# Expert gathers shifted from the V stages to the U stages, and ten modulation parts made inside the first layer's attention

## The chip, the core and the metric

The kernel runs on one core of one Trainium2 chip. The metric is device time in microseconds (us), the median of several runs. The core's engines work side by side: TensorE (PE in the rows; PEld is its weight loads) multiplies matrices, VectorE (DVE) and ScalarE (ACT) do elementwise work, GpSimd (POOL) does some elementwise work and here issues the indirect loads, and SyncE (SP) issues nearly all other transfers. Each engine takes its instructions strictly in the order in which they were placed, and waits where one is not ready. Sixteen DMA engines move data between the chip's memory and the on-chip buffers; they are shared by all transfers.

## What is computed

The program is two layers of a generator with 512 latent and 256 context tokens of width 1024. Cut to what matters here:

```
for l in range(2):
    mod = silu(c) @ w_mod[l] + b_mod[l]          # six parts of 1024: sh1 sc1 g1 sh2 sc2 g2
    h   = rms_norm(x) * norm_mix * (1 + sc1) + sh1
    y   = concat(windowed attention A, neighbourhood attention B, RWKV-7 scan C)(h @ w_in) @ w_out
    x   = x + g1 * y
    h2  = rms_norm(x) * norm_ffn * (1 + sc2) + sh2
    # PEER: 8 heads, each picks 16 of 16384 experts per token
    act = gelu(h2 . u[expert])
    x   = x + g2 * sum(gate * act * v[expert])
```

In layer 0 the context tokens (256) go through all of it too, in layer 1 only latent tokens do. Each of the six parts is made for `c` and for `c_ctx`, so one part needs a 1024 x 1024 slice of `w_mod` (4 MB) and little arithmetic.

## The kernel before

The tokens lie in six tiles of 128: LAT = 0 to 3, CTX = 4 and 5. A layer runs through `project` (norm, input projection), `mix` (scan, attention, output projection) and `peer`.

`peer` treats most tokens densely: for every one of the 16384 experts. The U stage goes through 128 blocks of 128 experts, two blocks (a pair) per row of `uT` (1 MB): `pa = u . h2`, 48 matmuls a pair, split into high and low parts (`uH`, `uL`, `hH`, `hL`) for precision. Between the pairs it makes the gate matrix W (`choose`, then `gates`: 32 steps a token tile, each two `oh` and one `og` on VectorE, eight `pw` matmuls and one copy), stored through `wscr`. The gate work of all tiles has to end at group GSPREAD of 32, since its buffers then make room for the results of the last blocks (`late`). The V stage goes through the same blocks again: `y += (gate * act) . v`, 64 pairs of a 1 MB row of v each. I call these stages U0, V0 (layer 0) and U1, V1 (layer 1).

The remaining tokens (CTX in layer 0, LAT tile 3 in layer 1) are not done densely: class `Gather` fetches the chosen expert rows. A gather is one indirect DMA on GpSimd's queue that brings one row of u and v for each of 128 tokens (1 MB). Two gathers together are then worked off by VectorE (L1464, the product with h; L1470, the sum into `accc`). There are 256 gathers in layer 0 and 128 in layer 1. They share six buffers (`row`) with the rows of `uT` and v. When a gather is placed is set by `tick`, called once per pair: every call adds NTICK[layer][place] to a sum, and each whole unit of it places one gather with high priority. The places are 0 (five calls in `scores`), 1 (U stage, groups below NFIRST), 2 (U stage, from NFIRST on), 3 (V stage). What is left at the end of the V stage is placed by `flush`.

`mod_unit` makes one modulation part: eight loads `wmod` of 512 KB, 32 small matmuls, a bias and, for the parts that the norms use, a transpose. In layer 0 parts 0 and 1 are made first in `project`, parts 2 to 5 behind them, with lower priority. Parts 0 and 1 of layer 1 are made in layer 0's `attention`, by `fill`, called once per head step there (a head step is one call of `soft`: 48 in layer 0, 8 for A on CTX, 8 for B on CTX, 16 for B, 16 for A on LAT; B on CTX does not call `fill`). Parts 2 to 5 of layer 1 are made in layer 1's `project`.

The order on every engine is not written by hand: the instructions are placed when the program is built, in the order in which a model of the chip finds them ready, highest priority first. So a change of one number moves instructions elsewhere too. In `mix` of layer 0 the context's output projection and its PEER choice (`outproj_ctx`, `peer_ctx`) have a higher priority than attention, which fills in between, and the latent output projection (`outproj`) needs all of attention.

Of the kernel before, what the change touches and what calls it, by code (L numbers as in the profile page):

```python
# [16 lines left out]
PSUM = bass.MemoryType.PSUM  # L17
# [17 lines left out]
LATER = 2000  # L35
NROW = 6
NQ = 2
MOFF = 500
GSPREAD = (24, 20)
LATE = (28, 28)  # L40
NM1 = 2
NMW = (6, 4)
NRAW = 4
TC0 = 6
NPSC, NPSL = 2, 4
# [9 lines left out]
NPRT = 4  # L55
NQKB = {"qs": 3, "kh": 3, "kl": 2}

NTICK = ((1, 1.0, 1.5, 2.4), (0, 0, 1.06, 1.06))
NFIRST = (12, 3)
FEATS = (12, 13, 4, 0, 5, 1, 6, 2, 7, 3, 14, 8, 9, 10, 11)  # L60
LAT = (0, 1, 2, 3)
# [5 lines left out]
class Kernel:  # L67
    nw = 0

    def __init__(self, ctx, tc, i, out, dbg):  # L70
        self.ctx, self.tc, self.nc, self.i, self.out, self.dbg = ctx, tc, tc.nc, i, out, dbg
        self.cp = ctx.enter_context(self.pool(name="cp", bufs=1))
        self.mods = list(range(NM1))

        self.xsb = {}
        self.consts()
        self.scratch()
# [150 lines left out]
    def project(self, l, st):  # L228
        tc, nc, i = self.tc, self.nc, self.i
        wc = l == 0  # L230
        cpl = self.colp[l]
        hp_ = st.enter_context(self.pool(name="hp", bufs=1))
        hH = hp_.tile([P, KC, T], F32R, name="hH")
        hL = hp_.tile([P, KC, T], F32R, name="hL")
        def mods(chunks):
            if s3.pools is None:
                s3.pools = [s3.enter_context(self.pool(name="mp", bufs=NMW[l], side="right")),
                            s3.enter_context(self.pool(name="mps", bufs=2, space=PSUM, side="right"))]
            self.mod(l, chunks, *s3.pools)

        def src(t):
            if l == 0:
                return i["x"][t * P:(t + 1) * P] if t < 4 else i["ctx"][(t - 4) * P:(t - 3) * P]
            return self.xp[t * P:(t + 1) * P]
        with ExitStack() as s3:
            s3.pools = None
            if l == 0:
                mods(range(2))
            with ExitStack() as s2:
                np_ = s2.enter_context(self.pool(name="np", bufs=2))  # L250
                nps = s2.enter_context(self.pool(name="nps", bufs=2, space=PSUM))
                mc = self.mcol[:, l, 0]
                for tiles in (CTX, LAT[:2], LAT[2:]):
                    self.norm_T(src, mc, hH, hL, tiles, np_, nps)
            if l:
                self.gat.close()
            with self.tc.high_priority(offset=-MOFF):
                mods(range(NM1 if l else 2, 6))
        ps = st.enter_context(self.pool(name="pps", bufs=2, space=PSUM))
        psn = st.enter_context(self.pool(name="psn", bufs=2, space=PSUM, side="right"))  # L260
        xp_ = st.enter_context(self.pool(name="xp", bufs=1, side="right"))
        win = i["w_in"][l].rearrange("(k p) n -> p k n", p=P)
        pre = st.enter_context(self.pool(name="pre", bufs=1)).tile([P, KC, 256], F32, name="pre")
        with ExitStack() as s2:
            b2 = s2.enter_context(self.pool(name="b2", bufs=2))
            pb = s2.enter_context(self.pool(name="pb", bufs=1))
            with self.tc.high_priority(offset=PREO):
                nc.sync.dma_start(pre, win[:, :, QKV0:QKV0 + 256])
            last = self.features(l, s2, win, hH, hL, ps, psn, xp_, b2, pb)
        with ExitStack() as s2:  # L270
            self.qkv(l, s2, win, hH, hL, ps, psn, pre)
        last()
# [291 lines left out]
    def attention(self, l, st):  # L564

        nc, i = self.nc, self.i
        wc = l == 0
        ap = st.enter_context(self.pool(name="ap", bufs=1))
        a2 = st.enter_context(self.pool(name="a2", bufs=2))
        psl = st.enter_context(self.pool(name="psl", bufs=NPSL, space=PSUM))  # L570
# [4 lines left out]
        mp = st.enter_context(self.pool(name="mp", bufs=2))  # L575

        def fill():
            if self.mods:
                self.mod_unit(1, self.mods.pop(0), mp, psl, "pl")

        def soft(parts, h, use_sink):

# [62 lines left out]
        def heads_A(tiles, lat):  # L645
            k0_ = 0 if lat else NLAT
            q0 = tiles[0] * P
            for e in range(2):
                o = a2.tile([P, NLAT], F32, name="o")[:, :len(tiles) * P]
                hd = load_k(2, e, k0_)  # L650
                qs = [load_q(z, e, q0, (tiles[-1] + 1) * P) for z in range(2)]
                for a, t in enumerate(tiles):
                    k0, k1 = max(0, t - 1), min(3, t + 1)
                    nk = (k1 - k0 + 1) * P if lat else 0
                    vals = [va[:, 4 + z, e * 64:e * 64 + 64] for z in range(2)]
                    if lat:
                        vals = [va[:, z, e * 64:e * 64 + 64] for z in range(k0, k1 + 1)] + vals
                    prTs = []
                    for z in range(2):
                        pl = psl.tile([P, 512], F32, name="pl")  # L660
                        parts = [(pl, nk + 256)] if nk <= 256 else [(pl, nk), (psl.tile([P, 512], F32, name="pl"), 256)]
                        pc, n = parts[-1]
                        q = qs[z][:, a * P:(a + 1) * P]
                        qk_mm(pc[:, n - 256:n], q, hd, lambda x: x[:, NLAT - k0_:])
                        if lat:
                            qk_mm(pl[:, 0:nk], q, hd, lambda x: x[:, k0 * P:(k1 + 1) * P])
                            if k0 < t:
                                nc.vector.tensor_tensor(pl[:, 0:P], pl[:, 0:P], am[:, 0], OP.add)
                            if k1 > t:
                                nc.vector.tensor_tensor(pl[:, nk - P:nk], pl[:, nk - P:nk], am[:, 1], OP.add)  # L670
                        fill()
                        prTs.append(soft(parts, 2 * e + z, True))
                    weigh(pl, prTs, [vals] * 2, o[:, a * P:(a + 1) * P])
                keep(e, o, q0)
# [5 lines left out]
        if wc:  # L680
            heads_A(CTX, False)
            for c in range(2):
# [3 lines left out]
                for a in range(2):  # L686
                    prTs = []
                    for z in range(2):
                        pl = psl.tile([P, 512], F32, name="pl")
# [15 lines left out]
        for c in range(2):  # L705
            o = a2.tile([P, NLAT], F32, name="o")
            qs = [load_q(3 + c, z, 0, NLAT) for z in range(2)]
            hd = [load_k(5 + c, z, 0) for z in range(2)]
            for j in range(4):
                prTs = []  # L710
                for z in range(2):
                    h = 2 * c + z
                    bias = a2.tile([P, 256], F32, name="bias")
                    nc.sync.dma_start(bias, i["rpb"][l, h, :, j])
                    nc.gpsimd.tensor_tensor(bias, bias, bm[:, j], OP.add)
                    pl = psl.tile([P, 512], F32, name="pl")
                    qb = a2.tile([P, P], F32R, name="qb")
                    nc.gpsimd.tensor_copy(qb.rearrange("p (r w) -> p r w", w=16),
                                          qs[z].rearrange("p (r w) -> p r w", w=64)[:, :, 16 * j:16 * j + 16])
                    qk_mm(pl[:, 0:256], qb, hd[z],  # L720
                          lambda x: x[:, :NLAT].rearrange("p (r w) -> p r w", w=64)[:, :, reg[j]:reg[j] + 32])
                    qk_mm(pl[:, 256:512], qb, hd[z], lambda x: x[:, NLAT:])
                    nc.vector.tensor_tensor(pl[:, 0:256], pl[:, 0:256], bias, OP.add)
                    fill()
                    prTs.append(soft([(pl, 512)], h, False))
                weigh(pl, prTs, [[vb[:, j, y, h * 64:h * 64 + 64] for y in range(2)] +
                                 [vc[:, y, h * 64:h * 64 + 64] for y in range(2)] for h in (2 * c, 2 * c + 1)],
                      o.rearrange("p (r w) -> p r w", w=64)[:, :, 16 * j:16 * j + 16])
            keep(2 + c, o, 0)
# [691 lines left out]
class Gather:  # L1421
# [51 lines left out]
    def tick(self, z):  # L1473
        self.due += NTICK[self.l][z]
        while self.due >= 1 and self.todo:
            self.due -= 1
            with self.K.tc.high_priority(offset=100000):
                self.gather(*self.todo.pop(0))
# [75 lines left out]
```

## Time and profile before

| | us |
|---|---|
| median of three runs | 5100.41 (5096.14 to 5110.7) |
| profiled execution, its own time | 5089.21 |
| span of the profiled execution | 5087.4 |
| PE busy in the span | 4438.3 (87%) |
| DVE busy in the span | 3738.1 (73%) |

The profiled execution lies 11.2 us below the median, and 1.8 us of its time lie outside the span. From the span's start the stages lie about as follows (read from the trace): projection of layer 0 to 510, scan to 727, attention and the context's part beside it to 995, `outproj` and `scores` to 1150, U0 to 2062, V0 to 2839, projection of layer 1 from 2885, scan to 3574, attention to 3640, U1 to 4520, V1 to 5080.

### The profile page before, as it was taken

What the parts mean: (1) busy time and instruction counts of PE and PEld (TensorE: products, weight loads), DVE (VectorE), ACT (ScalarE), POOL (GpSimd) and SP (SyncE); (2) the same over time, 40 slices, a digit from 0 to 9 for tenths busy, and PEclk for the clock granted to TensorE, in tenths of its full rate; (3) what the DMA queues carried; (4) which work ended last, traced back from release to release, by engine and by line L of the source; (5) the groups of instructions that cost most, each with busy time, mean ns of one, the idle gap of its engine ahead of it and who ended that gap; (6) DMA issues with size and microseconds to landing.
All of it is one profiled execution on the core that took longest, in us unless ns stands there. A gap on an engine that the chain in (4) does not pass through costs nothing. (4 is left out here: it accounts for less than half of the span.)

```text
span 5087.4 us, 74067 instructions
## 1 busy us (share of the span) xinstructions
PE 4438.3 (87%) x27525; PEld 3679.1 (72%) x27525; DVE 3738.1 (73%) x7611; ACT 1731.5 (34%) x2881; POOL 1338.2 (26%) x1403
## 2 busy tenths in 40 slices
PE   7778797689999979898889596799698998988999
PEld 4558666567888867787777364687578997977887
DVE  3964658869967754798888867758589877556887
ACT  3433234333333322222222244324333443332333
POOL 0536632011111111232222235455011111112121
PEclk9779887799999989999999787779799998999999
DMA  7434665235777755899999942573424887567998
GB/s 273 134 104 125 190 203 177 90 128 197 250 260 283 281 217 214 305 372 371 367 364 368 349 162 87 131 204 111 157 100 170 305 296 278 215 236 256 342 357 299
DMA packets 573865, 1186.55 MB, mean 233 GB/s; under 512 B 63152, under 2 KB 376384, under 8 KB 520768
## 3 DMA queue, kind: packets, MB, share of 16 engines
q1 hardware_dynamic: 507072, 758.39, 44.8%
q0 software_dynamic: 61440, 418.41, 22.1%
q10 hardware_dynamic: 4992, 5.02, 0.3%
q8 instruction: 216, 3.54, 0.3%
q14 instruction: 145, 1.19, 0.1%
HBM read 1005.19 MB, written 176.50 MB: 232 GB/s over the span
## 5 line engine op out<-in xcount | busy, mean ns | idle before, releaser
L1453 POOL DMA_INDIRECT row<-in_uv,eidx x384 | 580.2, 1511 | 2465.2 <-DVE accc L1470 1369.1
L136 PE MATMUL pa<-hH,uL 128*128 128x512 f32 (+1 forms) x2048 | 757.9, 370 | 36.0 <-DVE uL L1313 35.9
L134 PE MATMUL pa<-hH,uH 128*128 128x512 f32 (+1 forms) x2048 | 754.5, 368 | 25.8 <-ACT ar L1317 21.6
L135 PE MATMUL pa<-hL,uH 128*128 128x512 f32 (+1 forms) x2048 | 752.4, 367 | 0.0
L135 PE MATMUL py<-vL,GH 128*128 128x512 f32 x1792 | 705.9, 394 | 26.6 <-DVE vL L1365 26.5
L136 PE MATMUL py<-vH,GL 128*128 128x512 f32 x1792 | 698.4, 391 | 0.0
L134 PE MATMUL py<-vH,GH 128*128 128x512 f32 x1792 | 625.2, 397 | 67.5 <-ACT vH L1363 44.1
L1464 DVE SCALAR_TENSOR_TENSOR row<-row,h2c 128x1024 f32<-128x1024 f32 x384 | 467.6, 1220 | 293.6 <-DMA row<-in_uv,eidx 293.3
L1470 DVE SCALAR_TENSOR_TENSOR accc<-row,dt,accc 128x1024 f32<-128x1024 f32 x384 | 491.6, 1280 | 5.4
L1311 ACT CAST uH<-row 128x1024 fp32r<-128x1024 f32 x256 | 268.5, 1050 | 653.7 <-PE pa L135 582.2
L136 PEld LDWEIGHTS pa<-hH,uL 128*128 128x128 f32 x2048 | 391.4, 191 | 84.8 <-DVE uL L1313 45.8
L134 PEld LDWEIGHTS py<-vH,GH 128*128 128x128 f32 x1792 | 340.9, 191 | 148.6 <-ACT vH L1363 53.4
L134 PEld LDWEIGHTS pa<-hH,uH 128*128 128x128 f32 x2048 | 391.6, 191 | 66.6 <-ACT ar L1317 22.2
L135 PEld LDWEIGHTS pa<-hL,uH 128*128 128x128 f32 x2048 | 390.9, 191 | 39.4
L135 PEld LDWEIGHTS py<-vL,GH 128*128 128x128 f32 x1792 | 341.3, 190 | 105.6 <-DVE vL L1365 34.5
L1313 DVE TENSOR_TENSOR uL<-row,uH 128x1024 fp32r<-128x1024 f32 x256 | 311.8, 1220 | 128.4 <-ACT uH L1311 127.5
L136 PEld LDWEIGHTS py<-vH,GL 128*128 128x128 f32 x1792 | 339.6, 189 | 70.7
L1370 ACT CAST GH<-G 128x512 fp32r<-128x512 f32 (+1 forms) x256 | 145.0, 567 | 637.7 <-PE py L135 414.9
L1365 DVE TENSOR_TENSOR vL<-row,vH 128x1024 fp32r<-128x1024 f32 x256 | 309.4, 1218 | 26.5 <-ACT vH L1363 26.5
L1363 ACT CAST vH<-row 128x1024 fp32r<-128x1024 f32 x256 | 262.5, 1043 | 41.7 <-DMA row<-in_uv 23.1
L1239 PE MATMUL pw<-og,oh 128*128 128x128 f16 x1792 | 237.7, 297 | 33.5 <-DVE og L1234 23.5
L1231 DVE TENSOR_TENSOR oh<-iota,ix 128x512 f16<-128x512 f16 x448 | 170.5, 419 | 104.8 <-PE pw L1239 103.9
(385 smaller groups left out, 8577.1 us busy)
## 6 DMA issues: line engine op xcount, KB each, us to landing
row<-in_uT SPq DMA_DIRECT2D x128, 1024.0 KB
row<-in_uv SPq DMA_DIRECT2D x128, 1024.0 KB
wscr<-W SPq DMA_DIRECT2D x28, 2048.0 KB
wmod<-in_w_mod SPq DMA_DIRECT2D x96, 512.0 KB
wt<-wscr SPq DMA_DIRECT2D x32, 1024.0 KB
row<-in_wq SPq DMA_DIRECT2D x24, 1024.0 KB
ascr<-aw SPq DMA_DIRECT2D x96, 256.0 KB
av<-ascr SPq DMA_DIRECT2D x48, 512.0 KB
```

Source lines behind the costliest of these rows:

```text
L134: mm(out, lh, rh, start=first, stop=False)
L135: mm(out, lh, rl, start=False, stop=False)
L136: mm(out, ll, rh, start=False, stop=last)
L1231: nc.vector.tensor_tensor(oh[:, z], self.iota4, ix[:, z, tt].unsqueeze(1).to_broadcast([P, P, 4]), OP.is_equal)
L1239: nc.tensor.matmul(pw[:, q], oh[:, 1, :, q], og[:, z, :, q], start=z == 0, stop=z == 1)
L1311: nc.scalar.copy(uH, ur)
L1313: nc.vector.tensor_tensor(uL, ur, uH.bitcast(F32), OP.subtract)
L1363: nc.scalar.copy(vH, vr)
L1365: nc.vector.tensor_tensor(vL, vr, vH.bitcast(F32), OP.subtract)
L1453: self.K.nc.gpsimd.indirect_dma_start(out=r, out_offset=None, in_=self.K.i[f"uv{self.l}"], in_offset=bass.IndirectOffsetOnAxis(ap=self.idx ...
L1464: nc.vector.scalar_tensor_tensor(rows[z][:, 0:D], rows[z][:, 0:D], 1.0, self.h[:, a], OP.mult, OP.mult, accum_out=dt[:, z:z + 1])
L1470: nc.vector.scalar_tensor_tensor(acc, v, dt[:, z:z + 1], acc, OP.mult, OP.add)
```

## The change

Four things change. The rates of the gathers: layer 0 from (1, 1.0, 1.5, 2.4) to (2, 1.8, 2.1, 1.9), layer 1 from (0, 0, 1.06, 1.06) to (0, 0, 1.2, 1.0). The modulation parts 2 to 5 of layer 0 are no longer made in `project` but at the first four calls of `fill`. All six parts of layer 1 are made in layer 0's attention, one at every third call (NMA = 3). `project` of layer 1 makes none.

```diff
-MOFF = 500
-NM1 = 2
-NMW = (6, 4)
+NMA = 3
-NTICK = ((1, 1.0, 1.5, 2.4), (0, 0, 1.06, 1.06))
+NTICK = ((2, 1.8, 2.1, 1.9), (0, 0, 1.2, 1.0))
 (in __init__)
-        self.mods = list(range(NM1))
+        self.mods = [(0, c) for c in range(2, 6)] + [(1, c) for c in range(6)]
+        self.fills = 0
 (in project)
-        def mods(chunks):
-            if s3.pools is None:
-                s3.pools = [s3.enter_context(self.pool(name="mp", bufs=NMW[l], side="right")),
-                            s3.enter_context(self.pool(name="mps", bufs=2, space=PSUM, side="right"))]
-            self.mod(l, chunks, *s3.pools)
         with ExitStack() as s3:
-            s3.pools = None
-            if l == 0:
-                mods(range(2))
+            if wc:
+                self.mod(l, range(2), s3.enter_context(self.pool(name="mp", bufs=6, side="right")),
+                         s3.enter_context(self.pool(name="mps", bufs=2, space=PSUM, side="right")))
 ...
-            with self.tc.high_priority(offset=-MOFF):
-                mods(range(NM1 if l else 2, 6))
 (in attention)
         def fill():
-            if self.mods:
-                self.mod_unit(1, self.mods.pop(0), mp, psl, "pl")
+            self.fills += 1
+            if self.mods and (self.mods[0][0] == 0 or self.fills % NMA == 0):
+                self.mod_unit(*self.mods.pop(0), mp, psl, "pl")
```

In attention `wmod` has two buffers, in `project` it had six (layer 0) and four (layer 1).

Lines of the changed kernel are numbered up to nine lower than before. Three places show what the new order is.

VectorE at the end of V0, before. L1365 makes the last `vL`, L1464 and L1470 work off gathers, L1409 is the first step of the stage's end.

```order
L1365 TENSOR_TENSOR vL<-row,vH 128x1024 x2
L1470 SCALAR_TENSOR_TENSOR accc<-row,dt,accc 128x1024
L1464 SCALAR_TENSOR_TENSOR row,dt<-row,h2c 128x1024 x2
L1467 TENSOR_TENSOR dt<-dt,gatec 128x2
...
L1409 TENSOR_TENSOR yt<-py_18527,row 128x512
```

The same place in the changed kernel (L1357 is the last `vL`, L1391 and L1392 end the gathered tokens, L1401 is the first step of the dense ones).

```order
L1462 SCALAR_TENSOR_TENSOR accc<-row,dt,accc 128x1024
L1364 TENSOR_TENSOR GL<-G,GH 128x512
L1357 TENSOR_TENSOR vL<-row,vH 128x1024
L1391 TENSOR_TENSOR accc<-accc,row 128x1024 x2
L1392 TENSOR_TENSOR row<-row,accc 128x1024 x2
L1401 TENSOR_TENSOR yt<-py_19037,row 128x512
```

Before, 21 gathers of layer 0 are summed behind the last `vL`; in the changed order none is.

VectorE in U0 where the gate work ends (group 24 of 32), before: between two `uL` (L1313) of the last blocks stand 12 gate steps (L1231 twice, L1234 once) and two pairs of gathers, of which this is the end.

```order
L1231 TENSOR_TENSOR oh<-iota_64,ix 128x512 x2
L1234 TENSOR_TENSOR og<-oh,g_15971 128x1024
L1467 TENSOR_TENSOR dt<-dt,gatec 128x2
L1470 SCALAR_TENSOR_TENSOR accc<-row,dt,accc 128x1024 x2
L1464 SCALAR_TENSOR_TENSOR row,dt<-row,h2c 128x1024
L1313 TENSOR_TENSOR uL<-row,uH 128x1024 x5
```

The same place in the changed kernel: between two `uL` (L1305) stand 36 gate steps and five pairs of gathers. These rows are from its middle: the gates of the last token tile (`g_16391`) begin only here.

```order
L1305 TENSOR_TENSOR uL<-row,uH 128x1024
L1223 TENSOR_TENSOR oh<-iota_64,ix 128x512 x2
L1226 TENSOR_TENSOR og<-oh,g_14870 128x1024 x2
...
L1462 SCALAR_TENSOR_TENSOR accc<-row,dt,accc 128x1024
L1209 TENSOR_SCALAR gt<-pkT 128x128
...
L1226 TENSOR_TENSOR og<-oh,g_16391 128x1024 x2
L1462 SCALAR_TENSOR_TENSOR accc<-row,dt,accc 128x1024 x2
...
L1305 TENSOR_TENSOR uL<-row,uH 128x1024 x3
```

By the count of all rows, VectorE has 39 gate steps and 16 gathers from pair 48 to pair 52 of U0, and before 16 steps and 7 gathers; in all of U0 132 gathers against 90, in V0 114 against 145 (behind its pair 16: 88 against 114).

TensorE at the end of the context's expert scores (`pS`), before. L608, L617, L642 and L643 are head steps of A.

```order
L642 MATMUL pl<-kh,qs 128x384
L643 MATMUL pl<-kl,qs 128x384
L1129 MATMUL pS<-kt,qT 128x128 x2
L608 MATMUL pl<-c_ident,pr 128x128 x8
L642 MATMUL pl<-kh,qs 128x256
L643 MATMUL pl<-kl,qs 128x256
L617 MATMUL pl<-prT,va 64x128 x8
```

The same place in the changed kernel. L160 is a modulation part (`wmod`), L634 with `qb` a head step of B.

```order
L160 MATMUL pl<-wmod,cs 32x256 x7
L600 MATMUL pl<-c_ident,pr 128x128 x2
L1121 MATMUL pS<-kt,qT 128x128 x2
L609 MATMUL pl<-prT,vb 64x128 x4
L609 MATMUL pl<-prT,vc 64x128 x4
L160 MATMUL pl<-wmod,cs 32x256 x4
L160 MATMUL pl<-bmod,cs 32x256 x4
L176 MATMUL pl<-c_ident,rmod 128x128 x2
L634 MATMUL pl<-kh,qb 128x256
```

Counted on VectorE, 5 of the 48 head steps begin behind the last of the context's candidate searches before, and 22 in the changed kernel. In layer 1, 8 head steps begin behind the scan's last step before, and 3 in the changed kernel.

## Rows read from the trace of the kernel before

**Rows 1.** The page: share of the DMA engines and GB/s in 40 slices of 127 us.

```profile
DMA  7434665235777755899999942573424887567998
GB/s 273 134 104 125 190 203 177 90 128 197 250 260 283 281 217 214 305 372 371 367 364 368 349 162 87 131 204 111 157 100 170 305 296 278 215 236 256 342 357 299
```

**Rows 2.** Stretches, matmuls on `py` alone: PE, PEld, DVE busy (times), clock, DMA, GB/s.

```profile
2062.00:2246.00 184.00, 176.13 (x768) 145.71 (x769) 0.00 (x0) 0.97 0.95 339
2246.00:2839.00 593.00, 541.41 (x2305) 436.78 (x2304) 0.00 (x0) 0.98 1.00 368
4770.00:5050.00 280.00, 280.00 (x1237) 231.94 (x1236) 0.00 (x0) 1.00 1.02 359
```

**Rows 3.** Stretches, line L1453 alone (gathers issued by POOL): busy (times), clock, DMA, GB/s.

```profile
2062.00:2246.00 184.00, 48.91 (x34) 0.97 0.95 339
2246.00:2839.00 593.00, 179.39 (x119) 0.98 1.00 368
```

**Rows 4.** Groups by form: times, busy, mean ns of one, idle before it and releaser.

```profile
L1470 DVE SCALAR_TENSOR_TENSOR accc<-row,dt,accc 128x1024 f32<-128x1024 f32 x384 | 491.6, 1280 | 5.4
L1464 DVE SCALAR_TENSOR_TENSOR row<-row,h2c 128x1024 f32<-128x1024 f32 x384 | 467.6, 1220 | 293.6 <-DMA row<-in_uv,eidx 293.3
...
L1231 DVE TENSOR_TENSOR oh<-iota,ix 128x512 f16<-128x512 f16 x448 | 170.5, 419 | 104.8 <-PE pw L1239 103.9
L1234 DVE TENSOR_TENSOR og<-oh,g 128x1024 f16<-128x1024 f16 x224 | 150.4, 684 | 0.0
```

**Rows 5.** End of V0, all engines: PE, PEld, DVE, ACT, POOL, clock, DMA, GB/s; then one form there.

```profile
2839.00:2885.00 46.00, 0.06 (x4) 0.09 (x8) 44.28 (x63) 1.64 (x7) 13.07 (x8) 0.53 0.91 340
...
L1409 DVE TENSOR_TENSOR yt<-py,row 128x512 f32<-128x512 f32 x8 | 5.1, 680 | 0.0
```

**Rows 6.** U0 in its middle and at the end of the gate work, all engines.

```profile
1430.00:1819.00 389.00, 389.00 (x2043) 323.44 (x2042) 281.92 (x469) 140.12 (x222) 52.27 (x41) 1.00 0.76 279
1819.00:1875.00 56.00, 27.65 (x176) 22.38 (x175) 35.09 (x65) 13.73 (x25) 7.71 (x5) 0.64 0.69 258
```

**Rows 7.** The same two stretches: `pa` alone (PE, PEld, ACT), then `pw` alone (PE, ACT).

```profile
1430.00:1819.00 389.00, 321.38 (x1346) 249.37 (x1346) 33.17 (x56) 1.00 0.76 279
...
1430.00:1819.00 389.00, 90.80 (x688) 50.56 (x86) 1.00 0.76 279
1819.00:1875.00 56.00, 17.13 (x128) 9.36 (x16) 0.64 0.69 258
```

**Rows 8.** Modulation in layer 0's attention, one part each: PE and PEld busy (times).

```profile
625.00:673.00 48.00, 6.49 (x64) 1.43 (x64) 0.93 0.83 242
673.00:697.00 24.00, 4.76 (x64) 1.36 (x64) 1.00 0.66 207
```

**Rows 9.** Modulation in the two projections: PE and PEld busy (times) on `wmod` alone.

```profile
50.00:75.00 25.00, 11.99 (x136) 3.09 (x128) 0.93 1.01 378
110.00:135.00 25.00, 7.22 (x88) 2.39 (x88) 0.94 0.81 291
...
2880.00:2915.00 35.00, 10.71 (x108) 2.60 (x112) 0.70 1.00 348
...
2955.00:3020.00 65.00, 12.60 (x134) 3.67 (x134) 0.87 0.66 232
```

**Rows 10.** Stretches beside attention: L590 alone (once per head step), then all engines.

```profile
727.00:757.00 30.00, 0.97 (x8) 0.66 0.86 265
...
932.00:995.00 63.00, 0.97 (x8) 0.57 0.06 18
3574.00:3640.00 66.00, 0.86 (x7) 0.62 0.63 214
...
727.00:757.00 30.00, 25.81 (x109) 16.24 (x109) 15.60 (x47) 12.81 (x30) 4.71 (x10) 0.66 0.86 265
...
800.00:858.00 58.00, 36.50 (x180) 24.65 (x178) 52.24 (x127) 32.08 (x65) 20.23 (x16) 0.60 0.64 219
...
932.00:995.00 63.00, 26.70 (x133) 18.65 (x133) 58.73 (x277) 25.15 (x55) 1.22 (x4) 0.57 0.06 18
```

## The prediction

> **What bounds the kernel now.** I read the page's 40 slices first, then the stretches of the stages that the change touches, then single lines in them. The slices show one place where the DMA engines are full for long: V0, with a share near 1 and 364 to 372 GB/s, while U0 before it moves 250 to 283 GB/s [rows 1]. TensorE's price per matmul shows what that costs. In V1 it has no gap: 1237 matmuls in 280 us, 0.226 us each. V0 from 2246 on needs 593/2305 = 0.257 us each; ahead of that, with the first 16 pairs' `aw` still on chip, 768 took 184 us, 10 us of it the start [rows 2]. So V0 is bound by transport, U0 by TensorE (busy all 389 us of its middle, VectorE 282 of them [rows 6]), and the heads of layer 0's attention by VectorE (52 of 58 us, then 59 of 63 [rows 10]). The change moves transport from the first to the second, and work into the third.
>
> **V0.** In its last 593 us 119 gathers were issued [rows 3] and 368 GB/s moved, so 218 MB. By the counted order 26 fewer gathers of 1.05 MB stand there (88 instead of 114): 191 MB, 519 us at 368 GB/s. TensorE's floor is 2305 x 0.226 = 521 us. Two equal limits do not mesh without loss; the lower bound is 521 us, the upper what a rate of 350 GB/s gives, 545. I take 533: **-60 us** (-72 to -48). VectorE does not take over: a gather costs it 1.28 + 1.22 = 2.5 us [rows 4], and it was busy less than now.
>
> On the ceiling the Trainium skill speaks with two voices. Its page HBM Reference, section Specifications (TRN2), says that a core streaming alone measures about 425 GB/s; by that the 218 MB need 513 us, V0 is not held by transport, and taking gathers out would give little. The page DMA: Bandwidth & Descriptors, section Where 436 GB/s comes from, names about 358 GB/s as the limit of one core's HBM side; by that the 191 MB need 533 us. The flat 364 to 372 GB/s at a full share [rows 1] stand with the second and 3% above it. The -60 us rest on neither.
>
> **The end of V0.** TensorE stands still from 2839 to 2885, VectorE busy 44 of these 46 us with the gathers left over [rows 5]. In the new order none is left behind the last `vL`. What remains is the dense end, eight `yt` and eight sums of 0.68 us, 11 us [rows 5], and the first norm, some 4: **-31 us** (-34 to -22).
>
> **U0.** It takes 42 more gathers, 105 us of VectorE. The danger is the place where the gate work must end. There TensorE waits for VectorE already: of the 56 us from 1819 on it spends 11 on `pa` and 17 on `pw` [rows 7]. Between two `uL` VectorE has 12 gate steps and 2 pairs of gathers; a step costs 2 x 0.419 + 0.684 = 1.52 us [rows 4], so 18 + 10 = 28 us. In the new order it has 36 steps and 5 pairs: 55 + 25 = 80 us, all between the same two `uL`, with no `pa` to run. That is +52 us. What the order gives back: 23 steps with 8 `pw` each no longer stand ahead of pair 48, where TensorE is the bound. A `pw` costs (389 - 1346 x 0.226)/688 = 0.123 us [rows 7], so -23 us. But VectorE's own load per pair rises there: in the 389 us it had 107 us free [rows 6], and most of the other 33 gathers (83 us) have to fit. VectorE would stand at 90 to 95%, waiting now and then for a gather to land, as the 293 us of such waits in all say [rows 4]; I charge 13 us for that, in bounds of 0 and 40. U0: **+42 us** (+10 to +75).
>
> **The first layer's attention.** Eight more parts are made here. TensorE's share is small, 4.8 to 6.5 us each; with two buffers one took 48 and one 24 us [rows 8]. Ten in a row so take 240 to 480 us, and each holds one of the four PSUM tiles that head steps need, so attention falls behind the context's part: 22 instead of 5 head steps begin behind the context's last candidate search, 17 more. No row shows 17 steps alone. The bounds per step: 30/8 = 3.8 us where VectorE was half free (15.6 us for 8 steps, 2 us each), 63/8 = 7.9 us where `choose` shared VectorE and the granted clock was 0.57 (TensorE mostly at 1.2 GHz, having had gaps), 66/7 = 9.4 us in layer 1 [rows 10]. The new tail has `choose` at its start and nothing at its end, so I take 5.6: 17 x 5.6 = 95 us (65 to 160). Relief: the same steps leave the stretch ahead, where VectorE was 90% busy at 800 to 858 [rows 10]; 17 x 2 = 34 us, of which I credit 33, in bounds of 0 and 45. The loads stand in SyncE's queue, so whatever is behind a `wmod` that waits for a buffer waits too: keys, `bias`, `wq`. I leave that in the upper bound. Attention: **+62 us** (+20 to +130); behind it waits `outproj`, and all of PEER.
>
> **The projections.** Layer 0 loses four parts: 12.0 + 7.2 us of TensorE [rows 9], of which the first stretch is partly the norm's wait: **-14 us** (-20 to -6). Layer 1 loses four: 10.7 + 12.6 us [rows 9], the first of them beside the norm, where VectorE sets the pace: **-14 us** (-22 to -6).
>
> **Layer 1's attention.** 3 instead of 8 head steps are left behind the scan. At 9.4 us [rows 10] five of them are 47 us, but `w_out` has to be loaded and split there too, and the scan takes the steps in. **-10 us** (-30 to +5). The gathers of layer 1 change nothing: V1 has no gap to win [rows 2].
>
> **Sum.** -60 - 31 + 42 + 62 - 14 - 14 - 10 = -25 us. On the profiled execution, 5089.2, that is 5064; its 11 us distance to the median carried over, **5075 us**.
>
> **Rivals.** *Slower: the tail of attention costs its upper price.* The place is between the context's scores and `outproj`; if a head step there costs 7.9 us [rows 10], the tail is 134 us instead of 95 and the sum is +14; at the 9.4 us of layer 1 it is +40, 5140 us. From 7.1 us a step on nothing is gained, from 8 on the kernel is measurably slower. For it: the clock of 0.57 and a TensorE that is busy 27 of 63 us say that latency, not work, sets the pace. Against it: both rows have other VectorE work in them (`choose`; the split of `w_out`).
> *V0 is not held by transport but by the six row buffers*, which gathers and v rows share. Then V0 gains only with the waits for buffers, about half, 30 us: sum +5, 5105 us. For it: in V1 a share of 1.02 goes with no loss at 359 GB/s [rows 2]. Against it: the flat rate. By the 425 GB/s on the Trainium skill's page HBM Reference (section Specifications (TRN2)) this rival would be the likely one; no slice of the trace moves at such a rate [rows 1].
> *The gate work's end is hidden.* If TensorE reaches the place later than VectorE, the 52 us are not paid: sum -77, 5023 us. For it: nothing in the rows but that the real order of arrival is not known. Against it: the same place costs TensorE 28 us of standing now [rows 7].
>
> **Chances.** Forecast 0.45, slower tail 0.23, row buffers 0.17, hidden gate work 0.15. About 15 us, 0.3%, is what a measurement can tell from no change. The forecast's own spread, 5040 to 5105, puts 0.30 of its 0.45 below 5085 and 0.15 within. With the hidden gate work, and 0.04 of the row buffers (where VectorE gains besides), faster has 0.49. The row buffers leave 0.11 inside, so same has 0.26. The tail and 0.02 of the row buffers make 0.25 slower. The range that leaves out a tenth at each end reaches from the hidden gate work to the dearer tail: 5025 to 5135 us.
>
> **What the new profile would show.** V0: 0.23 us per `py` matmul, below 370 GB/s, and TensorE idle for some 15 us behind the last. U0: a stretch of about 100 us near its third quarter with few `pa` and VectorE full of L1223 and L1226. Attention: `outproj`'s first matmul some 48 us later than now (995). Projections: no `wmod` in layer 1, `pf` starting about 7 us earlier in layer 0. Wrong would be: head steps at 4 us each in the tail (then faster than said), V0 still at 0.25 us per matmul, or waits of TensorE for `wmod` loads in the scan, which I priced at nothing.

## The result, and the profile after

The changed kernel takes 5175.6 us (median; 5167.6 to 5182.7) against 5101.0 before, measured beside it: ratio 1.0143, 95% interval 1.0122 to 1.0165. It is slower by 75 us. The forecast was 5075 us and a range of 5025 to 5135, so direction and range were wrong. The profiled execution took 5167.6 us, 78 more than that of before.

The page's slices (127 to 129 us each) answer to [rows 1].

```profile
DMA  4344667615778886678999933465434878577897
GB/s 159 111 123 134 183 201 233 211 64 187 249 270 315 322 318 244 223 265 280 360 366 359 344 119 111 118 183 158 160 106 157 306 290 299 214 269 263 313 347 255
```

U0 now moves up to 322 GB/s where 283 was the most, and V0's later slices 344 to 366. The dip at the end of U0 (244 and 223 in slices 16 and 17) was there before (217 and 214 in slices 15 and 16). New are the 265 and 280 behind it, where V0 begins: before, the dip was followed by 305 and 372.

Stages in us, one profiled execution each, between the first or last instructions named (pairs of U0 and V0 by `uL` and `vL` on VectorE, the rest on TensorE). "Rates" is the kernel before with the new gather rates alone, "parts" the changed kernel with the old rates, "4 buffers" the changed kernel with four buffers for `wmod`, "best" the last experiment.

| stage, up to | before | after | rates | parts | 4 buffers | best |
|---|---|---|---|---|---|---|
| last `pf` of projection 0 | 503 | 497 | 503 | 494 | 496 | 504 |
| end of the scan | 221 | 233 | 224 | 228 | 236 | 228 |
| first matmul of `outproj` | 270 | 395 | 270 | 396 | 319 | 271 |
| first `pa` | 133 | 140 | 142 | 131 | 141 | 132 |
| U0, pair 48 | 677 | 667 | 668 | 682 | 682 | 711 |
| pair 52 | 95 | 149 | 137 | 96 | 129 | 69 |
| last `pa` | 155 | 153 | 154 | 152 | 155 | 140 |
| V0, pair 16 | 180 | 209 | 206 | 186 | 206 | 177 |
| last `py` | 602 | 547 | 548 | 612 | 549 | 565 |
| first `pf` of layer 1 | 81 | 37 | 40 | 78 | 37 | 47 |
| last `pf` | 427 | 422 | 421 | 415 | 417 | 416 |
| first matmul of `outproj` | 294 | 260 | 268 | 275 | 274 | 256 |
| U1, V1 and the rest | 1447 | 1456 | 1457 | 1457 | 1456 | 1462 |

Attention lost 125 us, pairs 48 to 52 of U0 54, V0's first 16 pairs 29. V0's rest gained 55, its end 44, layer 1's attention 34.

**Attention.** Stretches of the changed kernel, L582 alone (once per head step; [rows 10] showed this line as L590); the last one is layer 1, behind the scan.

```profile
730.00:812.00 82.00, 1.29 (x11) 0.56 0.68 212
812.00:982.00 170.00, 1.25 (x9) 0.82 0.71 242
982.00:1125.00 143.00, 2.94 (x22) 0.63 0.22 69
3679.00:3709.00 30.00, 0.26 (x3) 0.62 0.92 312
```

The same, `wmod` alone (PE, PEld busy):

```profile
730.00:812.00 82.00, 17.76 (x144) 3.65 (x144) 0.56 0.68 212
812.00:982.00 170.00, 22.59 (x194) 5.31 (x194) 0.82 0.71 242
982.00:1125.00 143.00, 9.24 (x86) 2.28 (x86) 0.63 0.22 69
```

And its waits from 730 to 1125, for TensorE and for SyncE's queue (us in all, times, longest; L163 is the load of `wmod`):

```profile
PE pl L160 <- DMA wmod<-in_w_mod: 44.5, 27, 4.8
...
SPq L163 <- PE pl L160: 63.1, 37, 6.5
...
SPq L163 <- DMA wmod<-in_w_mod: 35.1, 20, 5.6
```

The stretches start at the scan's end, at the first matmul of `outproj_ctx`, behind the context's last `pq`, and end at `outproj`. Before they took 31, 169 and 70 us. So 73 us are the tail (22 instead of 8 head steps, 5.2 us for each of the 14 more), and 51 lie ahead of `outproj_ctx`: by the scan's end 6 head steps were begun where 12 had been, and 144 matmul rows of the parts (two for each matmul of the program) stand where none had been. The prediction counted its tail from another mark, the last of the context's candidate searches (937 us before, 988 after). Behind it 22 instead of 5 head steps begin, the 17 more that it named, and they take 137 us instead of 58: 79 us more, 4.6 a step.

The timeline of the changed kernel shows what stands ahead of `outproj_ctx`: TensorE first, then SyncE's queue (start, duration, count behind the x; in brackets the wait before it; L634 is a head step).

```profile
761.34 1.08 PE L160 MATMUL pl<-wmod,cs 128*32 128x256 f32 x8 [1.59 <-DMA wmod<-in_w_mod]
764.19 1.08 PE L160 MATMUL pl<-wmod,cs 128*32 128x256 f32 x8 [1.77 <-DMA wmod<-in_w_mod]
...
767.11 0.56 PE L634 MATMUL pl<-kh,qs 128*128 128x256 f32 x1
```

```profile
731.43 12.64 SPq L163 DMA_DIRECT2D wmod<-in_w_mod  x5
...
745.77 19.89 SPq L163 DMA_DIRECT2D wmod<-in_w_mod  x8
...
768.21 1.12 SPq L620 DMA_DIRECT2D qs<-qkT  x2
```

From 745 to 765 TensorE gets one slice of `w_mod` about every 2.8 us, multiplies it in 1.1 and stands for the next. SyncE issues 13 of these loads between 731 and 766, each when a buffer is free, and the queries and keys (`qs`, `kh`, `kl`) of the next head steps only behind them, from 768 on. So here both orders hold the head steps up, that of TensorE and that of the queue.

**U0 and V0.** All engines of the changed kernel in U0's middle, at the end of the gate work and behind V0 ([rows 5, 6]):

```profile
1556.00:1944.00 388.00, 382.18 (x1966) 316.95 (x1966) 318.14 (x521) 136.26 (x221) 86.24 (x58) 1.00 0.86 322
1944.00:2081.00 137.00, 79.06 (x465) 64.09 (x464) 88.83 (x168) 35.18 (x62) 15.65 (x11) 0.63 0.57 217
2991.00:3028.00 37.00, 15.74 (x53) 7.42 (x52) 27.56 (x68) 22.92 (x45) 3.84 (x4) 0.58 0.41 121
```

Of the 137 us of the second row TensorE spends 42 on 312 `pw` and 37 on `pa`, and stands for 58. Between the two `uL` that the prediction speaks of, all engines, before and after:

```profile
1834.00:1884.00 50.00, 22.32 (x127) 17.85 (x128) 26.23 (x51) 9.99 (x18) 4.57 (x3) 0.56 0.50 189
```

```profile
1958.00:2065.00 107.00, 49.16 (x322) 39.53 (x323) 72.39 (x147) 25.29 (x47) 12.09 (x8) 0.52 0.57 217
```

VectorE is busy 72 us there, and was 26 before (80 and 28 were worked out). `py` alone in V0 ([rows 2]):

```profile
2236.00:2455.00 219.00, 186.18 (x767) 150.18 (x768) 0.00 (x0) 0.93 0.81 276
2455.00:2991.00 536.00, 525.14 (x2305) 431.46 (x2304) 2.65 (x4) 1.00 0.97 350
```

Behind pair 16 a matmul costs 536/2305 = 0.233 us, with 83 gathers issued: 3% above TensorE's price of 0.226 in V1. Ahead of it 768 took 219 us where 184 had done.

### The profile page after: what moved, and what is told of

It is laid out like the page before. It is cut to its first block, busy times and chain, and to the rows that moved or that the text cites. A ratio compares the mean times of both kernels' runs of the same rounds, so it can differ in the third digit from the quotient of the medians.

```text
span 5165.8 us, 74069 instructions
## 1 busy us (share of the span) xinstructions
PE 4468.2 (86%) x27525; PEld 3685.3 (71%) x27525; DVE 3732.1 (72%) x7611; ACT 1713.9 (33%) x2869; POOL 1334.7 (26%) x1403
## 5 line engine op out<-in xcount | busy, mean ns | idle before, releaser
L133 PE MATMUL py<-vH,GH 128*128 128x512 f32 x1792 | 661.6, 394 | 32.0 <-ACT GH L1362 21.4
L1305 DVE TENSOR_TENSOR uL<-row,uH 128x1024 fp32r<-128x1024 f32 x256 | 311.4, 1218 | 108.9 <-ACT uH L1303 108.4
L1357 DVE TENSOR_TENSOR vL<-row,vH 128x1024 fp32r<-128x1024 f32 x256 | 309.8, 1218 | 9.6 <-ACT vH L1355 9.4
L1231 PE MATMUL pw<-og,oh 128*128 128x128 f16 x1792 | 238.6, 297 | 73.0 <-DVE og L1226 47.3
L1231 PEld LDWEIGHTS <-oh 128*128 128x128 f16 x1792 | 190.6, 120 | 111.7 <-DVE og L1226 67.1
```

What stands on the lines that cost most here:

```text
L133: mm(out, lh, rh, start=first, stop=False)
L1231: nc.tensor.matmul(pw[:, q], oh[:, 1, :, q], og[:, z, :, q], start=z == 0, stop=z == 1)
L1305: nc.vector.tensor_tensor(uL, ur, uH.bitcast(F32), OP.subtract)
L1357: nc.vector.tensor_tensor(vL, vr, vH.bitcast(F32), OP.subtract)
```

## The experiments

Ratios are to the kernel before, measured beside each, with 95% intervals. Every edit also places the order anew, so a difference holds for the edit together with the order that it brings.

**The two halves apart.** One kernel takes only the new NTICK, one keeps all but that.

```diff
-NTICK = ((1, 1.0, 1.5, 2.4), (0, 0, 1.06, 1.06))
+NTICK = ((2, 1.8, 2.1, 1.9), (0, 0, 1.2, 1.0))
```

> The kernel before with only the new gather rates (both layers); the modulation parts stay where they were. Theory A (the loss is made by the modulation parts in layer 0's attention; the gathers' own account is even): read off the two traces stage by stage, the gathers cost +7 us in the scores, +43 in U0, +10 in layer 1, and give -27 in V0 and about -35 behind it, sum -2 us: 5099 us, within 15 us of before. Rival B (the gathers make the loss, in U0 and in the first pairs of V0, and the modulation is even): 5140 us or more. By the prediction's own terms (-60, -31, +42) it would be -49: 5052 us.

Measured: 5049.2 us, 0.991 (0.9889 to 0.9932), 48 us faster. Both theories missed; the 5052 us by the prediction's own terms came out, by errors that cancel (see below).

> The changed kernel with the old gather rates, so only the modulation parts are moved. Theory A: outproj begins some 130 us later, layer 1 gives back about 49 us (its projection 14, scan and attention 35): +81 us, 5182 us. Rival B: within 25 us of before. By the prediction's terms (+62, -14, -14, -10) it would be +24: 5125 us.

Measured: 5207.8 us, 1.0222 (1.0202 to 1.0241), 111 us slower. The loss is wholly that of the parts. It is some 30 us larger than theory A said. In the profiled execution layer 1 gives back 31 us instead of 49, since part of the gain in its attention, which A gave to the parts, comes with the rates alone as well (294 to 268 us); another 16 us lie in V0, without an explanation. The halves add up to 63, the change to 75. They are not independent: each alone shortens layer 1's attention by 26 and 19 us, both by 34.

**What in the parts costs.** First the buffers.

```diff
-        mp = st.enter_context(self.pool(name="mp", bufs=2))
+        mp = st.enter_context(self.pool(name="mp", bufs=4))
```

> The changed kernel with four buffers instead of two for wmod in attention. Theory A1 (TensorE, in order, stands at wmod matmuls because two buffers let a load start only when the one before the last is used up): the waits of TensorE for wmod (38.9 us between 725 and 920) shrink to under 10, the 22 late head steps become about 8, outproj begins at most 40 us later than before: 5075 to 5100 us. Rival C (what counts are the 32 MB and 1152 matmuls of eight more parts, however they are buffered): outproj no more than 25 us earlier than in the changed kernel, 5150 us or more.

Measured: 5100.1 us, 1.0009 (0.9991 to 1.0027). Theory A1 holds for the greater part: 76 of the 125 us are gone (30 of them ahead of `outproj_ctx`, 48 behind the last `pq`), and the whole change is worth nothing instead of minus 75. Waits of that kernel from 732 to 1051, lines as above:

```profile
SPq L163 <- PE pl L160: 13.2, 15, 2.1
...
PE pl L160 <- DMA wmod<-in_w_mod: 6.1, 5, 2.6
```

49 us over the kernel before stay. Next the work was taken out in steps, with two buffers.

```diff
-        for k in range(KC):
+        for k in range(1 if tag == "pl" else KC):
```

> The changed kernel, but in attention every modulation part is made from only the first of its eight slices of w_mod (one load, four matmuls, and the bias): 70 of 80 loads are left out. Theories A1 and C: attention becomes at least as short as before, where two whole parts were made in it; outproj at 960 to 1000, the time 5025 to 5060 us. Rival D (not loads and matmuls cost the time, but the PSUM tile that each part holds and the order of head steps among the parts): outproj at 1050 or later, 5100 us or more.

Measured: 5042.7 us, 0.9887 (0.9866 to 0.9907), 252 us from scan to `outproj`. Rival D falls for short parts: ten tiles and ten short parts among the head steps cost nothing. That a full part, which waits for its loads, holds its PSUM tile longer and keeps head steps out in that way, was not tried.

```diff
-            for j in range(4):
+            for j in range(4 if tag == "pm" or k == 0 else 0):
```

> The changed kernel, two buffers for wmod, all 80 loads in attention, but of each part only the first slice is multiplied: 70 x 4 matmuls are left out. Theory A1 (the time is TensorE's, which stands in order at each matmul whose load is still under way): outproj begins by 1000, 5040 to 5060 us, as in the kernel with one slice. Rival T (the time is that of the transfers: 35 MB, and SyncE's queue, in which keys and the context's weights stand behind them): outproj at 1050 or later, 5110 us or more.

Measured: 5115.3 us, 1.0034 (1.0017 to 1.005), 330 us. Here rival T came out, and A1 alone does not explain the loss: without the matmuls, 65 us are gone, and 60 over the kernel before stay. So the loads cost by themselves, by their bytes or by their places in the queue:

```diff
             w = pool.tile([P, 1024], F32, name="wmod")
-            nc.sync.dma_start(w, src[:, k])
+            c8 = 1024 if tag == "pm" or k == 0 else 128
+            nc.sync.dma_start(w[:, :c8], src[:, k, :c8])
```

> As the kernel with all loads and a single multiplied slice a part, but the seven loads that nothing uses bring only an eighth of their columns: 80 loads as before, 70 of them 64 KB instead of 512 KB. That kernel took 330 us from the scan's end to outproj, the one without those loads 252. Theory Y (the bytes: keys, weights and the parts' first slices come late behind 36 MB): 250 to 275 us, 5040 to 5065 us. Theory N (the number of loads and their places in SyncE's queue): 310 us or more, 5095 us or more.

Measured: 5059.4 us, 0.9913 (0.989 to 0.9937), 279 us. It is mostly the bytes: the time is theory Y's, the stretch 4 us above its range. All engines of the kernel with full loads, then with small ones: scan, then attention up to `outproj`.

```profile
498.00:740.00 242.00, 188.25 (x2479) 157.13 (x2478) 131.58 (x225) 56.69 (x128) 123.94 (x148) 0.78 0.69 204
740.00:1070.00 330.00, 231.43 (x1373) 179.21 (x1372) 233.76 (x846) 128.55 (x269) 44.58 (x74) 0.70 0.61 195
```

```profile
495.00:721.00 226.00, 183.75 (x2523) 153.44 (x2523) 136.58 (x257) 62.42 (x149) 124.40 (x148) 0.86 0.59 167
721.00:1000.00 279.00, 210.79 (x1341) 165.28 (x1335) 219.43 (x802) 114.36 (x245) 41.73 (x74) 0.75 0.49 155
```

Over the whole stretch the DMA engines are not full in either, but this mean hides where the loads stand. The first 200 us of attention, with full loads and then with small ones:

```profile
740.00:940.00 200.00, 150.07 (x837) 113.61 (x837) 118.29 (x304) 74.11 (x142) 37.33 (x50) 0.66 0.89 282
```

```profile
721.00:921.00 200.00, 167.93 (x1062) 132.30 (x1057) 143.25 (x428) 83.36 (x176) 37.85 (x59) 0.77 0.63 200
```

Where the full loads stand, the DMA engines are 0.89 busy, and 0.19 in the 130 us behind. By the scan's end 6 head steps were begun with full loads, 13 with small ones. Whether the bytes cost by DMA engines that are nearly full, by keys that come late behind the loads or by the order, which is placed anew around them in each kernel, these runs do not separate. Down the row: 395 us, 330 without the matmuls, 279 without most bytes, 252 without the loads.

Whether SyncE's queue, standing at the loads, is what holds the keys up was tried by another queue, with two and with four buffers:

```diff
-            nc.sync.dma_start(w, src[:, k])
+            (nc.gpsimd if tag == "pl" else nc.sync).dma_start(w, src[:, k])
```

> The changed kernel, two buffers for wmod, but in attention the wmod loads are issued on GpSimd's queue instead of SyncE's. In the changed kernel SyncE's queue stands 98 us at these loads between 730 and 1125, waiting for a buffer (63 for TensorE, 35 for the load before), with keys and weights behind them; TensorE stands 45 us for loads. Theory S (what costs is SyncE's queue, standing at the loads): the 395 us from the scan's end to outproj fall to 340 or less, 5120 us or less. Theory A1 (what costs is TensorE, standing in order at the loads that two buffers let come late): 375 us or more, 5155 us or more.

Measured: 5193.6 us, 1.0179 (1.0159 to 1.0199), 417 us.

> The same with four buffers. With four buffers on SyncE's queue this stretch took 319 us, the queue stood 13 us and TensorE 6 us at loads; 49 us over the kernel before were left. Theory S: a little of it was the queue, 300 to 315 us, 5085 to 5100 us. Theory W (the rest is work: 320 more matmuls of the parts in the stretch, on the path, with a clock that does not rise): 319 us as on the other queue, 5100 us within 12.

Measured: 5128.8 us, 1.0045 (1.0033 to 1.0057), 329 us. Theory W's time is missed as well; 18 us lie in the scan (254 instead of 236). Theory S finds no support in these times: both are slower than on SyncE's queue. It isn't refuted, since GpSimd has work of its own there and stood instead, as its waits from 720 to 1110 say (two buffers; `qb` belongs to head steps):

```profile
POOL wmod L163 <- PE pl L160: 128.2, 43, 14.7
POOL qb L710 <- PE pl L635: 29.8, 12, 9.3
```

By the Trainium skill (page Trainium Kernel Development and Optimization, section Key Constraints), transfers issued from SyncE, ScalarE and GpSimd run on the same 16 engines, and spreading them over queues saves issue time only. The 417 and 329 us against 395 and 319 agree in so far as the other queue brought no gain.

**Half of the parts.** Parts 2 to 5 of layer 0 go back to `project`.

```diff
-        self.mods = [(0, c) for c in range(2, 6)] + [(1, c) for c in range(6)]
+        self.mods = [(1, c) for c in range(6)]
-                self.mod(l, range(2), ...)
+                self.mod(l, range(6), ...)
```

> The changed kernel with parts 2 to 5 of layer 0 made in project again (behind parts 0 and 1, six buffers), the six parts of layer 1 in attention with two buffers. Theory A1 (each load waited for costs alike): four of eight extra parts gone, half of the 125 us, project +7: about 5120 us. If only the first four parts cost (they come at the first four head steps, all at once): 5070 us or less. If only layer 1's parts cost, which lie beside the context's part: 5165 us or more.

Measured: 5125.5 us, 1.0052 (1.0038 to 1.0067); 331 us to `outproj`, projection 0 longer by 19. The time is the one that theory A1 gave: an extra part costs about 15 us (61 for four, 125 for eight).

**The gate work's pile.** From here on, the kernel before with new rates only.

```diff
-NTICK = ((1, 1.0, 1.5, 2.4), (0, 0, 1.06, 1.06))
+NTICK = ((1, 1.0, 2.4, 2.1), (0, 0, 1.2, 1.0))
```

> The kernel before with the new gather rates in layer 1 and (1, 1.0, 2.4, 2.1) in layer 0: fewer gathers in U0's first 24 pairs, more behind them, none left behind V0. In the placed order 3 instead of 30 gate steps stand between pair 50 and 51 of U0, and 97 instead of 87 gathers behind V0's pair 16. Theory P (the 137 us from pair 48 to pair 52 are the piled-up gate steps): that stretch falls from 137 to 95 us or less; V0 pays 2 us for each of 10 gathers, as between the two rates seen so far (602 to 548 us for 27 gathers), +20: 5049 - 42 + 20 = 5027 us, 5010 to 5040. Rival (the stretch is long because the buffers for the last blocks come free there, whatever stands in VectorE's order): it stays above 125 us, 5060 us or more.

Measured: 5001.9 us, 0.9804 (0.9772 to 0.9836). Theory P holds: pairs 48 to 52 take 80 us instead of 137. All engines there, with the rates of the change alone, then with these:

```profile
1807.00:1944.00 137.00, 89.67 (x500) 72.62 (x499) 95.39 (x176) 37.89 (x66) 18.68 (x14) 0.68 0.64 240
```

```profile
1851.00:1931.00 80.00, 62.79 (x312) 51.20 (x310) 55.19 (x86) 20.88 (x37) 18.08 (x12) 0.89 0.78 299
```

Not all of it is won: the gates that are no longer piled up are worked ahead of pair 48 (708 instead of 668 us), so U0 as a whole gains 13 where the sum had 42. V0's rest takes 20 more, as expected. The time is 25 us below the expectation all the same. The profiled execution, the slowest of the four, is 14 below it: V0's first 16 pairs (185 instead of 206), layer 1's attention (256 instead of 268) and `scores` (132 instead of 142) gave more than U0 fell short.

**V0's first pairs.**

```diff
-NTICK = ((2, 1.8, 2.1, 1.9), (0, 0, 1.2, 1.0))
+NTICK = ((2, 1.8, 2.1, 2.4), (0, 0, 1.2, 1.0))
```

> The kernel before with the new gather rates, but V0's rate as before (2.4 instead of 1.9 a pair), so the gathers end at V0's pair 51. Theory R (V0's first 16 pairs are 26 us slower in the changed kernel because at 1.9 gathers a pair both gathers of a pair free their buffers together, and VectorE stands at the next landing with vL behind it): these pairs fall from 206 to 185 us or less, the rest of V0 takes 540 to 565, the time 5020 to 5040 us. Rival (the rate is not the cause): they stay above 200 us, 5045 us or more.

Measured: 5068.0 us, 0.9939 (0.9918 to 0.996). The first 16 pairs fall to 184 us, as theory R says, so the rate is the cause. But the rest takes 580 us, where theory R had 540 to 565, and layer 1's attention 287 instead of 268, so the time missed its 5020 to 5040 and is no better than at 1.9. For the first 16 pairs, all engines at 1.9 (the changed kernel's rates alone) and at 2.4:

```profile
2097.00:2304.00 207.00, 176.68 (x738) 142.18 (x737) 147.69 (x205) 51.93 (x79) 48.00 (x31) 0.94 0.81 275
```

```profile
2105.00:2289.00 184.00, 165.02 (x721) 136.15 (x721) 156.49 (x219) 53.74 (x81) 49.02 (x35) 0.94 0.95 333
```

And the waits there of VectorE for landings and of TensorE for `vL`, at 1.9 and at 2.4 (where the second is not among them):

```profile
DVE row L1464 <- DMA row<-in_uv,eidx: 55.8, 14, 8.7
...
PE py L135 <- DVE vL L1365: 17.9, 8, 4.3
```

```profile
DVE row L1464 <- DMA row<-in_uv,eidx: 16.9, 10, 3.3
```

More gathers, more bytes, and less waiting. Every kernel here at 1.9 a pair takes 200 to 209 us for these pairs, every one at 2.1 to 2.4 takes 173 to 186. At 1.9 VectorE stands up to 8.7 us at a landing while `vL` of the next block is behind it in its order, and the DMA engines are 0.81 busy. I read this as a loop of buffer, landing and sum, not as a limit of transport, but no run shows the loop itself, and why 1.9 makes these waits and 2.1 does not is not settled.

**Better rates.** Two versions with fewer early gathers.

```diff
-NTICK = ((1, 1.0, 1.5, 2.4), (0, 0, 1.06, 1.06))
+NTICK = ((1, 0.8, 2.6, 2.1), (0, 0, 1.2, 1.0))
```

> The kernel before with the new rates in layer 1 and (1, 0.8, 2.6, 2.1) in layer 0: beside the version (1, 1.0, 2.4, 2.1), which took 5002 us, fewer gathers in U0's first 24 pairs and more in its last 12. The order puts no gate step between pairs 50 and 52, and 95 instead of 97 gathers behind V0's pair 16. If the piled gate steps were all of it: the stretch from pair 48 to 52 takes about 70 instead of 79 us, 4990 to 5000 us. Rival (VectorE is then full between pairs 24 and 48, and what is taken from the pile is paid there): within 8 us of 5002 or slower.

Measured: 4995.9 us, 0.9798 (0.9779 to 0.9816); pairs 48 to 52 take 69 us. The time lies in the ranges of both; the stages decide against the rival, since up to pair 48 this version took 703 us and the one before it 708. That it is not faster still lies in layer 1's attention, 289 us where the version before it had 256. So the last version differs by 0.05 in one rate (2.55 for 2.6), chosen by the placed order of layer 1's attention:

```diff
-NTICK = ((1, 0.8, 2.6, 2.1), (0, 0, 1.2, 1.0))
+NTICK = ((1, 0.8, 2.55, 2.1), (0, 0, 1.2, 1.0))
```

> The kernel before with the new rates in layer 1 and (1, 0.8, 2.55, 2.1) in layer 0, 0.05 less than the version that took 4996 us. In the placed order both leave no gate step between U0's pairs 50 and 52 and no gather behind V0, but TensorE has 3 instead of 35 rows of layer 1's attention behind the scan. Theory H (each head step left behind layer 1's scan costs some 9 us: 66 us for 7, 30 us for 3 in the traces so far): the stretch from the projection's end to outproj takes about 256 instead of 289 us, 4963 us, 4950 to 4980. Rival (the steps taken into the scan lengthen it by as much): 4985 us or more.

Measured: 4975.5 us, 0.9746 (0.9719 to 0.9772). L590 behind the scan of layer 1, first with 2.6, then with 2.55:

```profile
3462.00:3528.00 66.00, 0.86 (x7) 0.62 0.61 213
```

```profile
3485.00:3516.00 31.00, 0.25 (x3) 0.68 0.90 307
```

Theory H holds: 4 steps fewer, 35 us less, and the scan took 223 and 224 us, so the rival falls. The time is 13 us short of the expectation; in the profiled executions the norm ahead of the projection (47 instead of 40), the projection (416 instead of 410) and U1 (721 instead of 713) took something back. This version beats both kernels, by 2.5% and (by the two ratios) 3.9%, and makes every modulation part where the kernel before made it.

## Why the prediction was wrong

**Attention: the step that failed.** The term was +62 and is +125. Its two halves went opposite ways. The tail was sized too high: the 17 further head steps cost 4.6 us each instead of 5.6, 79 us instead of 95. But the relief of 33 us does not exist: by the same mark the stretch ahead grew by 46 us (up to `outproj_ctx` alone by 51). The prediction let the steps leave this stretch and put nothing in their place. In fact the parts stand in their place: `outproj_ctx` waits for head steps of the context, these for the parts ahead of them in TensorE's order and for keys behind the parts' loads in SyncE's queue, and the parts for loads that two buffers bring one every 2.8 us. The prediction had both pieces in hand and gave them away: the waits of TensorE for `wmod` loads "in the scan, which I priced at nothing" (10.6 us in the scan, 44.5 behind it), and the keys behind a `wmod` that waits, of which it says "I leave that in the upper bound". With four buffers, 76 of the 125 us go; without the matmuls and most bytes of the unused slices, all but 9.

**The tail as the rival.** The rival's sign came true and its mechanism did not: a further step costs 4.6 us by the prediction's count, below the 7.1 from which on it saw nothing gained. What the forecast missed lies ahead of the tail.

**U0: right, with some luck in the size.** Pairs 48 to 52 grew by 54 us for the +52 worked out, all of U0 by 42 for 42 (and `scores` by 7). With the rates alone they grew by 42 and U0 by 32; the rest comes only with the parts in place and is not explained. The kernel with 3 gate steps there instead of 30 shows that the pile makes the stretch; that most of it comes back ahead of pair 48 when it is spread belongs to it. The hidden-gate-work rival is out.

**V0: half right.** Behind pair 16 it gained 55 us for the 60 forecast, 0.233 us a matmul for "0.23". Missed was the first quarter, which the prediction took over unchanged though its rate fell from 2.4 to 1.9: +29 us. The waits for landings there resemble the row-buffer rival's mechanism, in a place where neither the forecast nor the rival had put it. The Trainium skill's page HBM Reference (section Specifications (TRN2)) gives about 425 GB/s for a core that streams alone, and by that figure this rival would have led. The traces do not show it: no slice of the changed kernel moved more than 366 GB/s, and over 40 us the kernel before reached 396.

**End of V0: right, sized low:** -44 for -31. (The trace of the kernel before has 17 gathers summed behind the last `vL`, and not 21: four were worked off ahead of U0.) **Projections:** -6 and -5 for -14 each. In layer 0 the scan's end, which alone passes it on, came 5 us later than before; in layer 1 the kernel with the parts alone gained 12 there.

**Layer 1's attention: right in kind, sized low.** The 9.4 us a step held (35 us for four steps); the charge of 37 us against it, for `w_out` and a longer scan, was not paid.

**Sum.** For the gathers alone the terms gave -49, and the run -48, but by errors that cancel: V0 32 us less, its end and layer 1 some 40 more. The parts were forecast at +24 and made +111. The whole was forecast at -25 and is +75: of these 100 us the attention term makes 63 and V0's first pairs 29. With the attention term as forecast the change would still not have gained; only with both would it have.

Open are 12 us more in pairs 48 to 52 with both halves than with the rates alone, and which part of the 49 us left with four buffers is bytes and which is matmuls.

## What to carry to other kernels

Idle engine time does not make a place free: before work is moved into a stage, ask how many buffers its loads have there and what stands behind a late load on the engine that uses it and in the queue that issues it, and read the share of the DMA engines where the loads will stand, not as the mean of the stage. When steps leave a stretch, write down what the order puts in their place before crediting relief. Where the order is placed by a model, a rate is judged by that order: gate steps between two named rows and head steps behind the scan told here where 57 and 35 us would go (at least 42 and 33 were expected), and a rate changed by 0.05 moved one of them.

## What the runs showed of the hardware

Loads that nothing used cost 51 us when they brought 512 KB each instead of 64, though the DMA engines were only 0.61 busy over the stretch: where the loads stood, the share was 0.89. With two buffers a slice of 512 KB reached TensorE every 2.8 us, and from 731 to 766 SyncE's queue issued no load of the head steps. On GpSimd's queue 57 such loads kept that engine busy for 31.6 us, 0.55 us each. And V0's first pairs ran 23 us faster with more gathers, at 333 instead of 275 GB/s.
